# A two-layer decoder trunk in float32 on one core: down products summed onto x in PSUM, ordinary work by readiness, held transposes, reused banks

## The chip, the core and the metric

The kernel runs on one core of a Trainium2 chip. The core has TensorE for matmuls (PE in the profile, its weight loads PEld), VectorE (DVE), ScalarE (ACT), GpSimd (POOL) and SyncE (SP), which issues most DMAs here. Each engine runs its own instructions in order and waits for the others by semaphores. Matmuls write to PSUM, which has eight banks of 128 partitions x 512 float32; the other data lie in SBUF. The metric is the time of one execution on the device in microseconds; a kernel's figure is the median of its runs. A profiled execution gives the trace. Its span runs from the first instruction of the program to the last.

## The reference

256 tokens (two blocks of 128), width 2048, two layers. Each layer:

```
h = rms_norm(x, norm1_g);  z = h @ w_in                    # 2048 x 3584
out_a = chunked_sgu(gelu(z[:, :2048]), ...)                # spatial gate in chunks of 128
out_b = swa_sink_attention(q, k, v, ..., sinks, rel_bias)  # window of 128
x = x + concat(rms_norm(out_a), rms_norm(out_b)) @ w_out
h2 = rms_norm(x, norm2_g)
x = x + (silu(h2 @ w_gate) * (h2 @ w_up)) @ w_down         # 2048 x 5632, 5632 x 2048
```

All is float32.

## The kernel before

Every weight matrix is read from memory once, in loads of 256 x 512 float32 (`raw`, 512 KB, six buffers, issued by SP). A load is split into two float32r parts: ACT casts it to `wh` (L95), DVE subtracts to get `wl` (L96). The activations are kept in split form too (`hT`, `aT`, `ext`: tiles with a high and a low half). A product of a weight piece is three matmuls of 128 x 128 by 512 (`mm3`, L133: high x high, high x low, low x high), added in a PSUM bank; `first` sets `start`, by which the bank is begun anew.

The part around the change is the feed-forward of each layer. The 5632 gate and up columns are 11 blocks of 512. Nine of them (`S_BLOCKS`, 2 to 10) go through `seven` (L564): a two by two block product made of seven products instead of eight. Its halves are token block and row parity; DVE makes sums of weight pieces (L590, L591, L596), and one sum is completed by a DMA from GpSimd that adds to its destination (L598). The seven products are summed in banks of the pool `pa` (five buffers): `m0` to `m4` first, in half units of six matmuls (`s_unit`), then, after ACT and DVE have combined those banks in SBUF (L606 to L615), two more in newly taken banks `n0` and `n1` (L618), which DVE adds to `m1` and `c21` (L628). Silu and a product give the two result tiles `sg`.

Blocks 0 and 1 go through `gate_up` (L651), two ordinary products of eight units each (a unit is one load and 12 matmuls, L138). `down` (L666) multiplies finished blocks by `w_down`: for each of four columns of 512 it sums the units of its blocks in two PSUM banks, one per token block (`dacc`, the only two buffers of pool `pd`; banks of `pa` once the last seven-product block is through), and DVE adds the banks to the residual `xres` in SBUF (L685). In the last layer the last such addition is followed by the DMA to the output; in the first layer the last one is followed by the next layer's norm (`norm_block`).

A finished block's `sg` tiles (pool `zp`, tag `z`, eight buffers) are turned for `down` by `act_T` (L550): four transposes on PE into one bank, a copy on ACT (L554) and a subtraction on DVE (L555) give one of two `aT` tiles (eight buffers). `later(delay, fn)` puts such work off until the counter `clock` has gone on by `delay`; a unit counts 1, a half unit 0.5.

The order of the two kinds of work is planned when the program is built. `debt` counts DVE's work in microseconds (`vec`: 1.14 for a split or a sum, 0.6 for a PSUM operation) less PE's (`pe`: 0.227 per matmul times `LOAD`). After each step of the seven-product stream the ordinary stream goes on while `debt` is positive (L701 to L703). The ordinary stream is a written list, `STD_ORDER` (L43). Where a `down` lacks the transposed tiles of one of its blocks it yields `False` (L669), and only seven-product work goes on. When the seven-product blocks are through, the rest of the ordinary stream runs alone. The framework orders each engine's instructions by these priorities and by its own estimate of when they are ready, so neighbours may change places.

Of the kernel before, what the change touches and what calls it, by code (L numbers as in the profile page):

```python
# [16 lines left out]
ALU = mybir.AluOpType  # L17
# [34 lines left out]

# [12 lines left out]
def trunk(ctx, tc, x, xt, w_in, w_out, w_gate, w_up, w_down, sgu_w, sgu_g, consts,  # L65
# [39 lines left out]
    def vec(n, cost=VEC):  # L105
        debt[0] += n * cost
# [7 lines left out]
    def later(delay, fn):  # L114
        pending.append((clock[0] + delay, next(serial), fn))
# [8 lines left out]
    def new_acc(pool=pa, tag="acc"):  # L124
        return [pool.tile([P, NB], F32, tag=tag, name=f"{tag}{t}") for t in range(NTOK)]
# [7 lines left out]
    def mm3(acc, ah, al, wh, wl, first, last):  # L133
        nc.tensor.matmul(acc, ah, wh, start=first, stop=False)  # L134
        nc.tensor.matmul(acc, ah, wl, start=False, stop=False)  # L135
        nc.tensor.matmul(acc, al, wh, start=False, stop=last)  # L136

    def unit(src, acts, acc, first, last):  # L138
        raw = raw_load(src, 2 if clock[0] < 4 else 1)
        wh, wl = split2(raw)  # L140
        for j in range(2):
            act, aj = acts[j]
            for t in range(NTOK):
                ts = slice(t * P, (t + 1) * P)
                mm3(
                    acc[t], act[:, 0, aj, ts], act[:, 1, aj, ts], wh[:, j, :], wl[:, j, :],
                    first and j == 0, last and j == 1,
                )
        pe(12)
        tick()  # L150
# [100 lines left out]
    for lay in range(L):  # L251
# [298 lines left out]
        def act_T(b, c, sg, pairs_f=pairs_f):  # L550
            ps = pm.tile([P, 2, SEQ], F32, tag="sm", name="ps_f")
            transpose_pair([sg[t][:, 2 * c * P : (2 * c + 2) * P] for t in range(NTOK)], ps)
            pair = tp.tile([P, 2, 2, SEQ], F32R, tag="aT", name="aT")
            nc.scalar.copy(pair[:, 0], ps)  # L554
            nc.vector.tensor_tensor(pair[:, 1], ps, f(pair[:, 0]), ALU.subtract)  # L555
            vec(1, VEC_P)
            pe(2)
            pairs_f.setdefault(b, []).append(pair)

        def act_later(b, sg, act_T=act_T):  # L560
            for c in range(2):
                later(2 + c, lambda c=c: act_T(b, c, sg))

        def seven(b, lay=lay, pairs2=pairs2, ext2=ext2, act_later=act_later):  # L564
            bank = [pa.tile([P, NB], F32, tag="acc", name=f"m{i}") for i in range(5)]

            def s_unit(raw, m, i, op, first, last):
                wh, wl = split2(raw)
                for j in range(2):
                    ah, al = (op(2 * i + j, h) for h in range(2))  # L570
                    mm3(bank[m], ah, al, wh[:, j, :], wl[:, j, :], first and j == 0, last and j == 1)
# [34 lines left out]
            m1 = zp.tile([P, NB], F32, tag="z", name="m1")  # L606
            nc.scalar.copy(m1, bank[0])
            u1 = zp.tile([P, NB], F32, tag="z", name="u1")
            nc.vector.tensor_tensor(u1, bank[3], m1, ALU.add)
            c22 = zp.tile([P, NB], F32, tag="z", name="c22")  # L610
            c21 = zp.tile([P, NB], F32, tag="z", name="c21")
            nc.vector.tensor_tensor(c21, bank[2], u1, ALU.add)
            nc.vector.tensor_tensor(c22, bank[1], c21, ALU.add)
            nc.vector.tensor_tensor(u1, bank[1], u1, ALU.add)
            nc.vector.tensor_tensor(u1, bank[4], u1, ALU.add)  # L615
# [10 lines left out]
            sg = [m1, c21]  # L626
            for t, m in ((0, m1), (1, c21)):
                nc.vector.tensor_tensor(m, bank[t], m, ALU.add)  # L628
                nc.scalar.activation(m, m, AF.Silu, scale=rstd2[t])
            for t, c in ((0, u1), (1, c22)):  # L630
                nc.vector.scalar_tensor_tensor(sg[t], c, nrstd2[t], sg[t], ALU.mult, ALU.mult)
            vec(4, VEC_P)
            act_later(b, sg)
            yield

# [27 lines left out]
            vec(NTOK, VEC_P)  # L663
            act_later(b, sg)

        def down(blocks, final, lay=lay, pairs_f=pairs_f, norm_block=norm_block, ss1=ss1, pairs1=pairs1):  # L666
            for n in range(ND):
                while any(len(pairs_f.get(b, [])) < 2 for b in blocks):
                    yield False  # L669
                acc = new_acc() if seven_done[0] else new_acc(pd, "dacc")  # L670
                for k, b in enumerate(blocks):
                    for c in range(2):
                        pair = pairs_f[b][c]
                        unit(
                            w_down[lay, b, n, c], [(pair, 0), (pair, 1)], acc,
                            k == 0 and c == 0, k == len(blocks) - 1 and c == 1,
                        )
                        yield True
                for t in range(NTOK):
                    parts = 2 if final and lay == L - 1 and n == ND - 1 else 1  # L680
                    w = NB // parts
                    for i in range(parts):
                        cs = slice(n * NB + i * w, n * NB + (i + 1) * w)
                        xs = xres[:, t, cs]
                        nc.vector.tensor_tensor(xs, acc[t][:, i * w : (i + 1) * w], xs, ALU.add)  # L685
                        if final and lay == L - 1:
                            nc.sync.dma_start(out[t * P : (t + 1) * P, cs], xs)
                    vec(1, VEC_P)
                if final and lay < L - 1:
                    norm_block(n, ss1, pairs1, lay + 1, C_G1)  # L690

        def std_stream(gate_up=gate_up, down=down):
            for k, (kind, what) in enumerate(STD_ORDER):
                if kind == "gu":
                    yield from gate_up(what)
# [102 lines left out]
```

## Time and profile before

| | us |
|---|---|
| median of 3 runs | 1981.08 |
| lowest, highest | 1977.15, 1983.19 |
| profiled execution | 1970.47 |
| its span | 1968.8 |
| matmuls, share of the span | 99% |
| ACT, share of the span | 60% |
| DVE, share of the span | 85% |

The granted clock of TensorE was 1.0 over the span. The shares of the slices show where the phases lie (each digit is a tenth of busy time in a fortieth of the span, 49 us):

```profile
PE   9999999999999999999999999999999999999999
DVE  6665689999999999999856666899999999999996
ACT  7565566555565565565656755665656555655563
DMA  9544557667767668668555355576686776686684
```

The stretches in which DVE has 8 or 9 are the two feed-forward phases, about 297 to 960 and 1277 to 1940 us. Rows of groups are read so: line, engine, operation, out<-in by the program's names, shape, count | busy time, mean of one in ns | idle time of the engine just before them, and what ended most of it. A matmul's end is modelled.

### The profile page before, as it was taken

The page shows a single profiled execution, that of the slowest core. Times are in us where ns is not written, and L with a number is a line of the kernel's source. Part 1 is how long each engine was busy: PE and PEld are TensorE (multiplying, and loading weights), DVE is VectorE, ACT ScalarE, POOL GpSimd, SP SyncE. Part 2 cuts the span into 40 slices and gives each one's busy share as a digit, 9 for nine tenths or more (in the row PEclk, how much of TensorE's full clock was granted, in tenths as well). Part 3 has the DMA queues.
Part 4 walks back from the last instruction along what each step waited for, and adds up shares of the span by engine and source line. Part 5 has one row for each costly group of instructions (what it writes and reads, how often), then busy time and mean ns, then how long its engine had stood idle before and what let it go on. Part 6 is the DMA issues. An engine that isn't in the chain of part 4 may idle for free.

```text
span 1968.8 us, 24956 instructions
## 1 busy us (share of the span) xinstructions
PE 1942.7 (99%) x8884; PEld 1586.9 (81%) x8884; DVE 1678.4 (85%) x1812; ACT 1175.8 (60%) x1489; POOL 115.5 (6%) x116
## 2 busy tenths in 40 slices
PE   9999999999999999999999999999999999999999
PEld 6788888778887878888887888878788878888887
DVE  6665689999999999999856666899999999999996
ACT  7565566555565565565656755665656555655563
POOL 0210000000000000000002000000000000000000
PEclk9999999999999999999999999999999999999999
DMA  9544557667767668668555355576686776686684
GB/s 354 188 144 153 189 171 243 206 204 245 231 220 244 221 212 258 220 223 259 202 202 195 127 170 178 178 253 193 214 258 213 225 254 206 210 279 203 221 270 141
DMA packets 117805, 422.20 MB, mean 214 GB/s; under 512 B 13104, under 2 KB 13744, under 8 KB 117680
## 3 DMA queue, kind: packets, MB, share of 16 engines
q1 hardware_dynamic: 105264, 375.52, 53.2%
q0 software_dynamic: 12416, 45.09, 12.3%
q8 instruction: 69, 1.13, 0.2%
q14 instruction: 56, 0.46, 0.1%
HBM read 418.47 MB, written 2.10 MB: 214 GB/s over the span
## 4 chain that ended last, share of the span: by engine, by line
PE 85%; DVE 6%; issue 3%; ACT 2%; DMA 2%; POOL 1%; SPq 0%; DVEq 0%; ACTq 0%; POOLq 0%
PE dacc L134 9%; PE dacc L135 9%; PE dacc L136 9%; PE acc L135 8%; PE acc L136 8%; PE acc L134 8%; PE m L135 7%; PE m L136 7%; PE m L134 7%; PE n L135 3%; PE n L136 3%; PE n L134 3%; DVE wl L96 3%; ACT wh L95 1%; DVE raw L596 1%
## 5 line engine op out<-in xcount | busy, mean ns | idle before, releaser
L95 ACT CAST wh<-raw 128x1024 fp32r<-128x1024 f32 (+1 forms) x778 | 799.9, 1049 | 627.4 <-DVE raw L590 227.3
L96 DVE TENSOR_TENSOR wl<-raw,wh 128x1024 fp32r<-128x1024 f32 (+1 forms) x778 | 927.0, 1217 | 154.5 <-PE acc L135 75.9
L134 PE MATMUL dacc<-wh,aT 128*128 128x512 f32 x608 | 237.0, 392 | 0.2
L135 PE MATMUL dacc<-wl,aT 128*128 128x512 f32 x608 | 237.0, 390 | 0.0
L136 PE MATMUL dacc<-wh,aT 128*128 128x512 f32 x608 | 236.7, 390 | 0.0
L135 PE MATMUL m<-wl,ext 128*128 128x512 f32 x576 | 227.5, 395 | 4.7 <-DVE wl L96 4.7
L134 PE MATMUL m<-wh,ext 128*128 128x512 f32 x576 | 226.8, 394 | 4.8 <-ACT wh L95 4.8
L136 PE MATMUL m<-wh,ext 128*128 128x512 f32 x576 | 224.5, 390 | 0.0
L96 DVE TENSOR_TENSOR wl<-t,wh 128x1024 fp32r<-128x1024 f32 x144 | 175.5, 1219 | 16.0 <-issue 7.0
L95 ACT CAST wh<-t 128x1024 fp32r<-128x1024 f32 x144 | 151.4, 1051 | 49.5 <-PE dacc L136 31.6
L134 PE MATMUL acc<-wh,hT 128*128 128x512 f32 x448 | 179.4, 403 | 0.8 <-ACT wh L95 0.6
L135 PE MATMUL acc<-wl,hT 128*128 128x512 f32 x448 | 176.4, 394 | 1.2 <-DVE wl L96 1.1
L136 PE MATMUL acc<-wh,hT 128*128 128x512 f32 x448 | 175.6, 392 | 0.0
L598 POOL DMA_DIRECT2D t<-in_w_gate_dram x72 | 61.6, 855 | 1373.3 <-DVE wl L96 719.4
L134 PE MATMUL acc<-wh,aT 128*128 128x512 f32 x352 | 139.1, 395 | 0.0
L136 PE MATMUL acc<-wh,aT 128*128 128x512 f32 x352 | 137.3, 390 | 0.0
L135 PE MATMUL acc<-wl,aT 128*128 128x512 f32 x352 | 137.3, 390 | 0.0
L134 PEld LDWEIGHTS dacc<-wh,aT 128*128 128x128 f32 x608 | 114.1, 188 | 25.6 <-DVE xres L685 2.3
L135 PEld LDWEIGHTS m<-wl,ext 128*128 128x128 f32 x576 | 108.1, 188 | 32.0 <-DVE wl L96 10.7
L135 PEld LDWEIGHTS dacc<-wl,aT 128*128 128x128 f32 x608 | 114.2, 188 | 24.1 <-DVE wl L96 0.8
L136 PEld LDWEIGHTS dacc<-wh,aT 128*128 128x128 f32 x608 | 114.2, 188 | 23.7
L134 PEld LDWEIGHTS m<-wh,ext 128*128 128x128 f32 x576 | 108.2, 188 | 29.8 <-ACT wh L95 7.7
(145 smaller groups left out, 2974.3 us busy)
## 6 DMA issues: line engine op xcount, KB each, us to landing
raw<-in_w_gate_dram SPq DMA_DIRECT2D x176, 512.0 KB, 5.4
raw<-in_w_up_dram SPq DMA_DIRECT2D x176, 512.0 KB, 4.2
raw<-in_w_down_dram SPq DMA_DIRECT2D x176, 512.0 KB, 4.9
raw<-in_w_in_dram SPq DMA_DIRECT2D x108, 512.0 KB, 4.1
t<-in_w_gate_dram POOLq DMA_DIRECT2D x72, 512.0 KB, 5.9
raw<-in_w_out_dram SPq DMA_DIRECT2D x64, 512.0 KB, 3.3
bias<-in_band_dram POOLq DMA_DIRECT2D x8, 512.0 KB, 4.9
xr<-in_xt_dram SPq DMA_DIRECT2D x8, 256.0 KB, 6.1
```

Source lines behind the costliest of these rows:

```text
L95: nc.scalar.copy(wh[:, j : j + step, :], src)
L96: nc.vector.tensor_tensor(wl[:, j : j + step, :], src, f(wh[:, j : j + step, :]), ALU.subtract)
L134: nc.tensor.matmul(acc, ah, wh, start=first, stop=False)
L135: nc.tensor.matmul(acc, ah, wl, start=False, stop=False)
L136: nc.tensor.matmul(acc, al, wh, start=False, stop=last)
L596: nc.vector.tensor_tensor(b12, b12, b22, ALU.add)
L598: nc.gpsimd.dma_start(t2, w_gate[lay, b, i, 1], accum_op=ALU.add)
```

## The change

Six things change, the first four in the feed-forward alone:

- Residual: at the start of each column of `down`, ACT copies `xres` into the two banks, and the column's matmuls are added onto it (`start` never set); at the end ACT copies the banks back to `xres`. DVE's addition goes.
- Order: `STD_ORDER` goes. The ordinary stream runs a `down` on up to three blocks whenever two or more are fully transposed (or all that remain are), else the next `gate_up`, else yields. `LOAD` goes from 0.95 to 0.93.
- Held transposes: at most eight `aT` tiles are live; a block's transposes wait in `held` until the last column of a `down` gives tiles back.
- Used banks: the last two of the seven products are added onto banks 0 and 2, so `n0`, `n1` and one addition go, and half units 2 and 4 change places.
- `raw` has seven buffers instead of six.
- The scratch of GpSimd's DMAs (`dynamic_dma_scratch_size`) is 4096 instead of 8192.

```diff
-STD_ORDER = (
-    ("gu", 0), ("down", (0, 2)), ("gu", 1), ("down", (1, 3, 4)), ("down", (5, 6, 7)), ("down", (8, 9)), ("down", (10,)),
-)
+GU_BLOCKS = tuple(b for b in range(NFF) if b not in S_BLOCKS)
+CHUNK = (2, 3)
+ACT_TILES = 8
-LOAD = 0.95
+LOAD = 0.93
...
-        raw = wp.tile([P, 2, NB], F32, tag="raw", name="raw", bufs=6)
+        raw = wp.tile([P, 2, NB], F32, tag="raw", name="raw", bufs=7)
...
+        held = []
+        live = [0]
+
+        def release(live=live, held=held, act_T=act_T):
+            while held and live[0] < ACT_TILES:
+                live[0] += 1
+                act_T(*held.pop(0))
+
-        def act_later(b, sg, act_T=act_T):
+        def act_later(b, sg, held=held, release=release):
             for c in range(2):
-                later(2 + c, lambda c=c: act_T(b, c, sg))
+                def ready(c=c):
+                    held.append((b, c, sg))
+                    release()
+
+                later(2 + c, ready)
...
+                s_unit(b22, 4, i, e_op(3), first, last)
+                yield
                 s_unit(b12, 2, i, e_op(0), first, last)
                 yield
-                s_unit(b22, 4, i, e_op(3), first, last)
-                yield
                 kept.append(t2)
...
+            nc.scalar.copy(m0, bank[0])
+            nc.vector.tensor_tensor(m0, bank[3], m0, ALU.add)
+            nc.vector.tensor_tensor(c12, bank[1], m0, ALU.add)
+            nc.vector.tensor_tensor(c12, bank[4], c12, ALU.add)
+            nc.vector.tensor_tensor(c21, bank[2], m0, ALU.add)
             nc.vector.tensor_tensor(c22, bank[1], c21, ALU.add)
...
-            bank = [pa.tile([P, NB], F32, tag="acc", name=f"n{i}") for i in range(2)]
             for i in range(4):
                 b21 = raw_load(w_gate[lay, b, i, 1])
-                first, last = i == 0, i == 3
-                s_unit(b21, 0, i, a_op(1, 0), first, last)
+                s_unit(b21, 0, i, a_op(1, 0), False, i == 3)
                 yield
-                s_unit(kept[i], 1, i, a_op(1, 1), first, last)
+                s_unit(kept[i], 2, i, a_op(1, 1), False, i == 3)
                 yield
...
+            nc.vector.tensor_tensor(m0, bank[2], m0, ALU.add)
+            sg = [zp.tile([P, NB], F32, tag="z", name="sg0"), m0]
+            for t, c in ((0, bank[0]), (1, m0)):
+                nc.scalar.activation(sg[t], c, AF.Silu, scale=rstd2[t])
...
+        left = [NFF]
+
+        def down(blocks, lay=lay, pairs_f=pairs_f, norm_block=norm_block, ss1=ss1, pairs1=pairs1, left=left, live=live, release=release):
+            left[0] -= len(blocks)
+            final = left[0] == 0
             for n in range(ND):
-                while any(len(pairs_f.get(b, [])) < 2 for b in blocks):
-                    yield False
                 acc = new_acc() if seven_done[0] else new_acc(pd, "dacc")
+                for t in range(NTOK):
+                    nc.scalar.copy(acc[t], xres[:, t, n * NB : (n + 1) * NB])
                 for k, b in enumerate(blocks):
                     for c in range(2):
...
+                        if n == ND - 1:
+                            live[0] -= 1
+                            release()
                         yield True
...
-                        nc.vector.tensor_tensor(xs, acc[t][:, i * w : (i + 1) * w], xs, ALU.add)
+                        nc.scalar.copy(xs, acc[t][:, i * w : (i + 1) * w])
...
+            gus = list(GU_BLOCKS)
+            downed = set()
+            while left[0]:
+                full = [b for b in sorted(pairs_f) if len(pairs_f[b]) == 2 and b not in downed]
+                rest = left[0] == len(full)
+                if len(full) >= CHUNK[0] or rest:
+                    blocks = full[: CHUNK[1]]
+                    downed.update(blocks)
+                    yield from down(blocks)
+                elif gus:
+                    yield from gate_up(gus.pop(0))
                 else:
-                    yield from down(what, k == len(STD_ORDER) - 1)
+                    yield False
...
-    nc = bacc.Bacc("TRN2", target_bir_lowering=False, num_devices=1, dynamic_dma_scratch_size=8192)
+    nc = bacc.Bacc("TRN2", target_bir_lowering=False, num_devices=1, dynamic_dma_scratch_size=4096)
```

More of the change, by code (lines that the diff above doesn't have):

```diff
@@ L131, in small_ps, with mm3, unit @@
         return pool.tile(shape, F32, tag=tag, name=name)
[L133 to L138, printed above, removed]
+    def mm3(acc, ah, al, wh, wl, first, last, again=False):
+        nc.tensor.matmul(acc, ah, wh, start=first, stop=False, skip_group_check=again)
+        nc.tensor.matmul(acc, ah, wl, start=False, stop=False, skip_group_check=again)
+        nc.tensor.matmul(acc, al, wh, start=False, stop=last, skip_group_check=again)
+    def unit(src, acts, acc, first, last, again=False):
         raw = raw_load(src, 2 if clock[0] < 4 else 1)
@@ L146, in unit @@
                     acc[t], act[:, 0, aj, ts], act[:, 1, aj, ts], wh[:, j, :], wl[:, j, :],
-                    first and j == 0, last and j == 1,
+                    first and j == 0, last and j == 1, again,
                 )
@@ L558, in act_T, with s_unit @@
             pairs_f.setdefault(b, []).append(pair)
-        def act_later(b, sg, act_T=act_T):
+        held = []
[5 more added lines that the diff above has]
+        def act_later(b, sg, held=held, release=release):
             for c in range(2):
-                later(2 + c, lambda c=c: act_T(b, c, sg))
+                def ready(c=c):
+                    held.append((b, c, sg))
+                    release()
+                later(2 + c, ready)
         def seven(b, lay=lay, pairs2=pairs2, ext2=ext2, act_later=act_later):
             bank = [pa.tile([P, NB], F32, tag="acc", name=f"m{i}") for i in range(5)]
-            def s_unit(raw, m, i, op, first, last):
+            def s_unit(raw, m, i, op, first, last, bank=bank):
                 wh, wl = split2(raw)
@@ L570, in s_unit @@
                     ah, al = (op(2 * i + j, h) for h in range(2))
-                    mm3(bank[m], ah, al, wh[:, j, :], wl[:, j, :], first and j == 0, last and j == 1)
+                    mm3(
+                        bank[m], ah, al, wh[:, j, :], wl[:, j, :], first and j == 0,
+                        last and j == 1, m in (0, 2),
+                    )
                 pe(6)
@@ L600, in seven @@
                 yield
+                s_unit(b22, 4, i, e_op(3), first, last)
+                yield
                 s_unit(b12, 2, i, e_op(0), first, last)
                 yield
-                s_unit(b22, 4, i, e_op(3), first, last)
-                yield
                 kept.append(t2)
[L606 to L609, printed above, removed]
@@ L610, in seven @@
-            c22 = zp.tile([P, NB], F32, tag="z", name="c22")
-            c21 = zp.tile([P, NB], F32, tag="z", name="c21")
-            nc.vector.tensor_tensor(c21, bank[2], u1, ALU.add)
+            m0, c12, c21, c22 = (
+                zp.tile([P, NB], F32, tag="z", name=v) for v in ("m0", "c12", "c21", "c22")
+            )
+            nc.scalar.copy(m0, bank[0])
+            nc.vector.tensor_tensor(m0, bank[3], m0, ALU.add)
+            nc.vector.tensor_tensor(c12, bank[1], m0, ALU.add)
+            nc.vector.tensor_tensor(c12, bank[4], c12, ALU.add)
@@ L623, in seven @@
                 yield
-                s_unit(kept[i], 1, i, a_op(1, 1), first, last)
+                s_unit(kept[i], 2, i, a_op(1, 1), False, i == 3)
                 yield
[L626 to L630, printed above, removed]
+            nc.vector.tensor_tensor(m0, bank[2], m0, ALU.add)
+            sg = [zp.tile([P, NB], F32, tag="z", name="sg0"), m0]
@@ L631, in seven @@
+            for t, c in ((0, bank[0]), (1, m0)):
+                nc.scalar.activation(sg[t], c, AF.Silu, scale=rstd2[t])
+            for t, c in ((0, c12), (1, c22)):
                 nc.vector.scalar_tensor_tensor(sg[t], c, nrstd2[t], sg[t], ALU.mult, ALU.mult)
-            vec(4, VEC_P)
+            vec(3, VEC_P)
             act_later(b, sg)
@@ L664, in gate_up @@
             act_later(b, sg)
-        def down(blocks, final, lay=lay, pairs_f=pairs_f, norm_block=norm_block, ss1=ss1, pairs1=pairs1):
+        left = [NFF]
+        def down(blocks, lay=lay, pairs_f=pairs_f, norm_block=norm_block, ss1=ss1, pairs1=pairs1, left=left, live=live, release=release):
+            left[0] -= len(blocks)
+            final = left[0] == 0
             for n in range(ND):
-                while any(len(pairs_f.get(b, [])) < 2 for b in blocks):
-                    yield False
                 acc = new_acc() if seven_done[0] else new_acc(pd, "dacc")
+                for t in range(NTOK):
+                    nc.scalar.copy(acc[t], xres[:, t, n * NB : (n + 1) * NB])
                 for k, b in enumerate(blocks):
@@ L675, in down @@
                             w_down[lay, b, n, c], [(pair, 0), (pair, 1)], acc,
-                            k == 0 and c == 0, k == len(blocks) - 1 and c == 1,
+                            False, k == len(blocks) - 1 and c == 1, True,
                         )
+                        if n == ND - 1:
+                            live[0] -= 1
+                            release()
                         yield True
+                last = final and lay == L - 1
+                parts = 2 if last and n == ND - 1 else 1
+                w = NB // parts
                 for t in range(NTOK):
-                    parts = 2 if final and lay == L - 1 and n == ND - 1 else 1
-                    w = NB // parts
                     for i in range(parts):
@@ L684, in down, with std_stream @@
                         xs = xres[:, t, cs]
-                        nc.vector.tensor_tensor(xs, acc[t][:, i * w : (i + 1) * w], xs, ALU.add)
-                        if final and lay == L - 1:
+                        nc.scalar.copy(xs, acc[t][:, i * w : (i + 1) * w])
+                        if last:
                             nc.sync.dma_start(out[t * P : (t + 1) * P, cs], xs)
-                    vec(1, VEC_P)
                 if final and lay < L - 1:
                     norm_block(n, ss1, pairs1, lay + 1, C_G1)
[L692 to L695, printed above, removed]
+        def std_stream(gate_up=gate_up, down=down, pairs_f=pairs_f, left=left):
+            gus = list(GU_BLOCKS)
[9 more added lines that the diff above has]
+                    yield from gate_up(gus.pop(0))
                 else:
-                    yield from down(what, k == len(STD_ORDER) - 1)
+                    yield False
         other = std_stream()
```

2 lines of the change are left out of this document (removed).

## The prediction

> **What bounds the kernel now.** I read the busy shares first, then the two long stretches in which the gated product and the down product run (a "feed-forward phase" per layer), then the pauses in them.
>
> ```profile
> PE 1942.7 (99%) x8884; PEld 1586.9 (81%) x8884; DVE 1678.4 (85%) x1812; ACT 1175.8 (60%) x1489; POOL 115.5 (6%) x116
> ```
>
> TensorE's matmul row is full to 1.3%. By the view of time windows (length, then busy time and count of PE, PEld, DVE, ACT, POOL):
>
> ```profile
> 297.00:960.00 663.00, 656.19 (x2908) 535.98 (x2907) 629.38 (x614) 397.18 (x422) 29.86 (x35) 1.00 0.72 230
> 1277.00:1940.00 663.00, 656.85 (x2912) 536.86 (x2912) 629.77 (x615) 397.97 (x423) 29.87 (x35) 1.00 0.72 230
> 420.00:540.00 120.00, 120.00 (x536) 98.63 (x535) 112.87 (x109) 70.73 (x76) 5.11 (x6) 1.00 0.68 217
> 392.00:406.00 14.00, 12.16 (x55) 9.29 (x54) 13.83 (x15) 8.52 (x11) 1.70 (x2) 1.00 0.65 186
> 588.00:604.00 16.00, 13.92 (x65) 10.72 (x64) 15.90 (x18) 9.92 (x13) 1.71 (x2) 1.00 0.60 161
> 1373.00:1387.00 14.00, 11.93 (x53) 8.88 (x53) 13.84 (x15) 8.53 (x11) 1.70 (x2) 1.00 0.57 176
> 1568.00:1584.00 16.00, 13.92 (x65) 10.67 (x64) 15.90 (x18) 10.02 (x12) 1.71 (x2) 1.00 0.62 171
> ```
>
> The first two rows are the phases: PE is idle 6.8 and 6.2 us in them, 13.0 in all. The third is a stretch with no idle. The last four hold 1.84 + 2.08 + 2.07 + 2.08 = 8.1 us of the 13.0, with DVE at 99%: there DVE is the bound. Elsewhere in the phases DVE is near 95% and PE full. What PE waited for inside one of them (timeline of PE):
>
> ```profile
> 595.62 0.27 PE L199 MATMUL ps_f<-ident,sg 128*128 128x128 f32 x1
> 596.44 0.49 PE L134 MATMUL m<-wh,ext 128*128 128x512 f32 x1 [0.54 <-ACT wh L95]
> 597.70 0.50 PE L135 MATMUL m<-wl,ext 128*128 128x512 f32 x1 [0.77 <-DVE wl L96]
> 598.04 0.39 PE L136 MATMUL m<-wh,ext 128*128 128x512 f32 x1
> 598.27 0.40 PE L134 MATMUL m<-wh,ext 128*128 128x512 f32 x1
> ```
>
> A matmul is shown 0.39 us long, but the next starts 0.23 us after it, so each pause is shown about 0.16 us too short. The Trainium skill ("Perfetto Trace Analysis", Identifying the Most-Contended Engine) says so more generally: the matmul row is a bad measure of nearness to the limit, the share of weight loads a better one. Taken alone, 81% would look like 19% of room; the stretch without idle has 98.63 / 120 = 82.2%, so the trace does not agree with that much.
>
> At 82.2% the weight loads of the two phases would take 535.98 / 0.822 = 652 and 536.86 / 0.822 = 653 us, which leaves 21 us of room; the four windows would then hold 2.7 + 3.0 + 3.2 + 3.0 = 11.9. So the whole room is 13 to 21 us, about 1%: the change neither adds nor removes a matmul, so nothing larger can be won by it in these phases.
>
> **The change part by part.**
>
> *Ordinary work by readiness.* The written order makes the ordinary stream stand still when `down((0, 2))` and `down((1, 3, 4))` come up right behind a `gate_up` whose transposes are still due 2 and 3 units later: `yield False`. I stepped the planner's sums by its own rule (1.14 per split or sum, 0.6 per PSUM operation, minus 0.227 x LOAD per matmul). Before: after 41 and again after 115 half units of a layer, six half units follow with no ordinary unit. Each half unit is 6 matmuls, 1.36 us of PE, while DVE's split of it takes 1.22 us (the row below) and the sums as much again. These are the four windows: the `ps_f<-ident,sg` in the rows above is that `gate_up`'s transpose. After: with one full block at the end of the first `gate_up`, the second one starts at once; behind it blocks 0, 2 and 3 are full and the first down runs on them. The stepped order is (0,2,3), (1,4,5), (6,7), (8,9), (10), with no such standstill.
>
> ```profile
> L96 DVE TENSOR_TENSOR wl<-raw,wh 128x1024 fp32r<-128x1024 f32 x774 | 924.3, 1219 | 152.7 <-PE acc L135 75.9 <-issue 34.6 <-ACT wh L95 21.0
> ```
>
> The work there is moved, not saved, but PE's total is fixed, so the idle goes: between 8.1 (as shown) and 11.9 (by weight loads); I take 10, between the two since each of the dozen pauses is shown 0.16 us short.
>
> Counted over a layer: a seven-product block leaves 51.6 - 172 x 0.2111 = 15.3 of debt and an ordinary unit repays 1.39 (before 15.1, 1.45, and 1.2 more debt for each finished column), so 101 of the 120 ordinary units run beside the nine blocks instead of 108, and 19 instead of 12 behind them. The 12 are confirmed by the trace:
>
> ```profile
> L134 PE MATMUL acc<-wh,aT 128*128 128x512 f32 x352 | 139.1, 395 | 0.0
> L685 DVE TENSOR_TENSOR xres<-dacc,xres 128x512 f32<-128x512 f32 x60 | 39.3, 682 | 0.5 <-PE dacc L136 0.2
> L685 DVE TENSOR_TENSOR xres<-acc,xres 128x512 f32<-128x512 f32 x18 | 12.3, 687 | 10.3 <-PE acc L136 10.3
> L685 DVE TENSOR_TENSOR xres<-acc,xres 128x256 f32<-128x256 f32 x4 | 1.4, 418 | 4.1 <-PE acc L136 4.1
> L628 DVE TENSOR_TENSOR m<-n,m 128x512 f32<-128x512 f32 x18 | 12.3, 682 | 0.0
> ```
>
> (352 less the 64 x 4 of the output projection is 96, four for a unit: 24 units in two layers.) The seven units moved behind cost nothing, since a stretch of ordinary units is bound by PE: 12 matmuls against one split.
>
> *Residual by PSUM.* DVE loses 39.3 + 12.3 + 1.4 = 53.0 us. ACT gets a copy in and a copy out for each half column: five down calls, four columns, two token blocks, two layers. No row shows SBUF to PSUM. The nearest:
>
> ```profile
> L554 ACT CAST aT<-ps_f 128x512 fp32r<-128x512 f32 x44 | 25.7, 583 | 20.1 <-PE ps_f L199 11.6 <-PE dacc L136 8.6
> L459 ACT CAST hT<-g 128x512 fp32r<-128x512 f32 x16 | 10.0, 623 | 0.5
> L656 ACT ACTIVATE sg<-dacc,ir 128x512 f32<-128x512 f32 x8 | 5.3, 688 | 4.6 <-PE dacc L136 4.6
> L134 PEld LDWEIGHTS dacc<-wh,aT 128*128 128x128 f32 x608 | 114.1, 188 | 25.6 <-DVE xres L685 2.3
> L134 PEld LDWEIGHTS dacc<-wh,hT 128*128 128x128 f32 x256 | 47.9, 188 | 12.8 <-ACT wh L95 2.4 <-ACT sg L656 0.7
> ```
>
> Out: 0.58 (L554, from PSUM); in: 0.58 to 0.62, I take 0.60. About 80 x 0.58 + 80 x 0.60 = 94 us, which brings ACT from 60% to 65%: no bound. The price is in the turn of a bank. A down column in the phase has only the two `dacc` banks, so column n+1 waits until column n is out. Before, its first bank came free 0.68 us after PE was done; now after out, out, in = 1.76, that is 1.1 later, and the casts of the next units stand behind these copies on ACT, DVE's splits behind the casts, PE behind both. By the stepping there are 13 such turns per layer, 26. They cost nothing while PE has half units ready; without that cover 1.1 each, 28.6 us. From below: the 2.3 us that L685 holds PE now goes too. The nearest rows: four turns behind ACT's Silu (L656) held PE 0.7 us, 0.18 each. I take 0.2 each, 5.2, less 2.3 = 2.9 lost. What speaks for a small price is that ACT may be late without harm; it waited 2.75 and 1.62 us for PE at two starts of L554, and in the window around them PE lost nothing (timeline of ACT, then the window):
>
> ```profile
> 706.94 0.59 ACT L554 CAST aT<-ps_f 128x512 fp32r<-128x512 f32 x1 [2.75 <-PE dacc L136]
> ...
> 711.05 0.59 ACT L554 CAST aT<-ps_f 128x512 fp32r<-128x512 f32 x1 [1.62 <-PE dacc L136]
> ...
> 704.00:716.00 12.00, 12.00 (x55) 9.91 (x56) 11.37 (x14) 6.21 (x8) 0.37 (x1) 1.00 0.91 279
> ```
>
> At the end of the kernel four half copies on ACT replace four adds of 0.42 us on DVE in front of the output's DMAs: within 0.2 us, nothing. SP's queue has these DMAs at the same places as before, the next loads behind them.
>
> *Held transposes* put a block's transposes off until fewer than eight `aT` tiles live; the L554 waits above are what they act on, hidden already. Where one is released, ACT's copy waits for the unit just issued, as in the last window: nothing on PE. Two `z` tiles per held block stay in use; the stepping has at most four held at once.
>
> *Products onto used banks.* One addition fewer per block (L628, 12.3 us in all), no banks `n`; the half units 4 and 2 change places, so that bank 2's sum is the fourth of five DVE operations, and two to three ordinary units and a half unit stand before the product that needs it. Nothing on PE.
>
> *Seven raw buffers.* The chain of waits has single loads of 7 us on it, issued only when a buffer came free:
>
> ```profile
> 368.50 0.36 ACT aT L554
> 368.86 7.08 DMA raw<-in_w_up_dram
> 376.04 1.06 ACT wh L95
> 377.14 0.50 PE dacc L134
> ```
>
> One more buffer issues each load a unit earlier. With the freed DVE time (65 us) it acts on the idle outside the four windows: 4.9 us as shown, 8.8 by weight loads. I take 3; the ends are 0 and 8.8. POOL's half scratch: its 72 accumulating loads stand far apart (POOL 6% busy), nothing.
>
> **Sum:** -10 - 3 + 2.9 = -10.1 us. The profiled execution took 1970.47 us, of which 1968.8 are the span; it would become 1960.4. The median of the runs is 1981.1, so 10.6 more than the profiled one; the same difference gives **1971.0**.
>
> **Rivals.**
>
> 1. *As summed*, 1966 to 1977.
> 2. *All the room is won*: turns hidden altogether (-2.3) and up to 15.7 of the 21 us: -18, 1963. For it: DVE would have 4% more slack everywhere. Against: some pauses lie at the phases' beginning, where no stock has been made yet.
> 3. *No change*: the pauses leave the four windows and come back at the 26 turns, at 0.5 to 0.6 us each: 26 x 0.55 - 2.3 = 12 against 13 won, 1980. For it: splits are ready shortly before PE needs them in these phases, and every turn puts 2.4 us of copies ahead of the next cast.
> 4. *Slower*: at each turn PE finds no half unit ready, and the whole 1.1 us shows: 28.6 - 2.3 - 13 = +13, 1994. It decides from 0.59 us a turn on; beyond 0.82 the loss exceeds 0.3%. Against it: window 704 to 716, and L656.
>
> **Numbers.** Chances: 0.45, 0.12, 0.26, 0.17. A measurement of this kernel tells 0.3% (5.9 us) from no change, so faster means under 1975.1 and slower over 1987. Faster: 0.41 of the first, the second, 0.03 of the third, 0.56. Slower: 0.15 of the fourth, rounded up to 0.16. The rest is 0.28. Range: 1960 (the second, less the runs' 3 us of scatter) to 1992, just short of the fourth's full price. The forecast's own range is 1966 to 1977.
>
> **What would show it.** Readiness right: no pair of windows per layer with DVE at 99% and PE idle by 2 us; PE idle in the phases under 6 us. Turns right: PE's waits for ACT's copies under 6 us in all, ACT near 65%, DVE near 82%. Loads right: no 7 us load in the chain. It would be wrong if PE's first matmul of a column waits half a microsecond or more for ACT in most turns, if DVE idles behind casts, or if the ordinary stream stands still elsewhere for want of full blocks.

## The result and the profile after

| | us |
|---|---|
| changed kernel, median of 4 runs | 1952.36 (1951.71 to 1953.42) |
| kernel before, beside it | 1979.99 (1977.15 to 1983.19) |
| ratio | 0.9861, 95% interval 0.9843 to 0.9878 |
| profiled execution after, and its span | 1952.96, 1951.2 |
| profiled execution before, and its span | 1970.47, 1968.8 |

The change is faster by 1.4%. Between the two medians lie 27.6 us, between the two profiled executions 17.5. The forecast was 10. Both differences matter below: the second is what the first traces can account for, the first is what the kernel gained.

The busy row of the changed kernel's page:

```profile
PE 1936.5 (99%) x8884; PEld 1587.5 (81%) x8884; DVE 1624.8 (83%) x1712; ACT 1253.2 (64%) x1651; POOL 115.3 (6%) x116
```

The same 8884 matmuls. DVE's row is 53.6 us shorter and ACT's 77.4 longer. Instructions of one engine overlap a little in the trace, so these rows show less than the sum of the instructions' own durations, which fell by 64.5 on DVE and rose by 93.9 on ACT: the 65 and 94 of the forecast. The windows of the two feed-forward phases, then the two stretches in which the transposes behind a `gate_up` now fall in the first layer:

```profile
297.00:960.00 663.00, 662.29 (x2948) 543.80 (x2947) 612.65 (x578) 434.86 (x495) 29.88 (x35) 1.00 0.75 233
1277.00:1940.00 663.00, 662.43 (x2948) 544.06 (x2947) 607.73 (x567) 434.07 (x493) 29.89 (x35) 1.00 0.73 229
389.00:403.00 14.00, 14.00 (x67) 11.57 (x67) 13.10 (x14) 7.14 (x9) 0.84 (x1) 1.00 0.83 257
484.00:500.00 16.00, 16.00 (x76) 13.22 (x75) 13.60 (x15) 10.30 (x13) 0.00 (x0) 1.00 0.65 220
```

PE's idle time in the phases went from 13.0 to 0.7 + 0.6 = 1.3 us. By weight loads at 82.2% (543.80 / 0.822 = 661.6 and 544.06 / 0.822 = 661.9) the room went from 21 to about 2.5. So what the first trace showed as room has been won nearly to the end, and DVE has slack (612.65 and 607.73 busy of 663, before 629 and 630). Who held PE's weight loads, and what ACT waited for among the loads from memory (waits from 297 to 1940 us, that is the phases and what lies between them):

```profile
PEld dacc L135 <- DVE wl L96: 6.8, 18, 0.4
PEld m L135 <- DVE wl L96: 2.3, 4, 1.0
...
PEld dacc L134 <- ACT dacc L686: 2.0, 6, 0.4
...
ACT wh L95 <- DMA raw<-in_w_down_dram: 2.2, 4, 0.8
...
ACT wh L95 <- DMA raw<-in_w_gate_dram: 0.6, 1, 0.6
```

The columns are microseconds in all, times, and the longest. The new copies (L686 in, L705 out) hold PE 2.0 us in all; the adds of before held it 2.3. ACT waited 2.8 us for loads; in the first profile of before it was 25.6:

```profile
ACT wh L95 <- DMA raw<-in_w_down_dram: 19.9, 20, 2.7
...
ACT wh L95 <- DMA raw<-in_w_up_dram: 4.3, 4, 1.4
...
ACT wh L95 <- DMA raw<-in_w_gate_dram: 1.4, 1, 1.4
```

### The profile page after: what moved, and what is told of

The parts are those of the page before. It is cut to its first block, busy times and chain, and to the rows that moved or that the text cites. A ratio compares the mean times of both kernels' runs of the same rounds, so it can differ in the third digit from the quotient of the medians.

```text
span 1951.2 us, 24946 instructions
## 1 busy us (share of the span) xinstructions
PE 1936.5 (99%) x8884; PEld 1587.5 (81%) x8884; DVE 1624.8 (83%) x1712; ACT 1253.2 (64%) x1651; POOL 115.3 (6%) x116
## 4 chain that ended last, share of the span: by engine, by line
PE 91%; DVE 3%; issue 3%; ACT 1%; DMA 1%; POOL 1%; SPq 0%; ACTq 0%; DVEq 0%; POOLq 0%
PE m L135 11%; PE m L136 11%; PE m L134 11%; PE dacc L135 10%; PE dacc L134 10%; PE dacc L136 10%; PE acc L135 8%; PE acc L136 8%; PE acc L134 8%; DVE wl L96 1%; PE ps_f L199 1%; POOL ir L182 1%; PE ps_v L372 1%; PE ps_n L199 1%; ACT s L349 0%
## 5 line engine op out<-in xcount | busy, mean ns | idle before, releaser
L135 PE MATMUL dacc<-wl,aT 128*128 128x512 f32 x576 | 225.9, 392 | 0.0
L136 PE MATMUL dacc<-wh,aT 128*128 128x512 f32 x576 | 225.0, 391 | 0.0
L134 PE MATMUL dacc<-wh,aT 128*128 128x512 f32 x576 | 224.3, 394 | 0.1
L134 PE MATMUL m<-wh,hT 128*128 128x512 f32 x432 | 168.4, 390 | 0.0
L136 PE MATMUL m<-wh,hT 128*128 128x512 f32 x432 | 168.3, 389 | 0.0
L135 PE MATMUL m<-wl,hT 128*128 128x512 f32 x432 | 168.3, 389 | 0.0
L134 PE MATMUL acc<-wh,aT 128*128 128x512 f32 x384 | 151.5, 395 | 0.0
L136 PE MATMUL acc<-wh,aT 128*128 128x512 f32 x384 | 150.1, 391 | 0.0
L135 PE MATMUL acc<-wl,aT 128*128 128x512 f32 x384 | 149.7, 390 | 0.0
L135 PEld LDWEIGHTS dacc<-wl,aT 128*128 128x128 f32 x576 | 108.2, 188 | 26.4 <-DVE wl L96 4.7
L134 PEld LDWEIGHTS dacc<-wh,aT 128*128 128x128 f32 x576 | 107.8, 188 | 25.2 <-ACT dacc L686 2.0
```

The costliest lines, as they stand in the source:

```text
L134: nc.tensor.matmul(acc, ah, wh, start=first, stop=False, skip_group_check=again)
L135: nc.tensor.matmul(acc, ah, wl, start=False, stop=False, skip_group_check=again)
L136: nc.tensor.matmul(acc, al, wh, start=False, stop=last, skip_group_check=again)
```

## The experiments

Runs of one group share the runs of the kernel before on the same chip. "Difference" is median less the median of before in the group; the changed kernel was run again in the second group.

| run | difference, us | ratio to before, 95% interval |
|---|---|---|
| e1 before again | 0.1 | 0.9999 (0.9990 to 1.0008) |
| e2 order and held transposes alone | -16.0 | 0.9917 (0.9903 to 0.9931) |
| e3 residual alone | +5.2 | 1.0022 (1.0011 to 1.0032) |
| e4 changed kernel, written order | -8.3 | 0.9955 (0.9942 to 0.9969) |
| e5 changed kernel | -24.8 | 0.9873 (0.9858 to 0.9888) |
| e6 changed kernel, residual on DVE | +0.5 | 1.0005 (0.9996 to 1.0014) |
| e7 changed kernel, six raw buffers | -14.9 | 0.9921 (0.9908 to 0.9934) |
| e8 changed kernel, banks n again | -24.3 | 0.9877 (0.9862 to 0.9892) |
| e9 as e6, LOAD 0.95 | -14.9 | 0.9925 (0.9913 to 0.9937) |
| e10 seventh raw buffer alone | -10.2 | 0.9953 (0.9941 to 0.9964) |
| e11 changed kernel, LOAD 0.95 | -16.9 | 0.9914 (0.9901 to 0.9928) |
| e12 held transposes alone | -1.5 | 0.9995 (0.9986 to 1.0003) |
| e13 order, held transposes, seventh buffer, halved scratch | -24.5 | 0.9877 (0.9858 to 0.9896) |
| e14 as e6, LOAD 0.945 | -20.8 | 0.9897 (0.9878 to 0.9917) |
| e15 changed kernel, LOAD 0.92 | -22.5 | 0.9891 (0.9871 to 0.9910) |
| e16 halved scratch alone | -0.4 | 0.9997 (0.9986 to 1.0008) |
| e17 changed kernel, eight raw buffers | -21.3 | 0.9889 (0.9875 to 0.9904) |

Some expectations, printed below, missed. e6 fits neither of its two theories, and e9 and e14 lie between theirs. e3, e4, e7 and e17 lie 1 to 4 us outside the range that fits them best, and e15 went the other way, within the intervals. e5 was expected at 1946 to 1950 us and took 1951.9; its four runs lie within 1.6 us of each other, the 17 of before beside it within 6.8.

### e1: the kernel before, again

No edit.

> The kernel before, unchanged. Asked: is the profiled execution's 1970.5 us, 10 us under its median, a lucky one? If the pauses of the two phases vary from execution to execution (theory V), this profile shows a span apart from 1968.8 by several us, with other pauses in the four windows at 392, 588, 1373 and 1568 us. If the trace is the same within 1 us and the runs are again near 1980, the profiled execution is simply shorter than the others for a reason that lies outside the pauses.

Its 11 runs lay between 1973.54 and 1977.54, and the other runs of before in the later groups between 1971.81 and 1984.28. The 1970.47 of the first profile is the shortest execution of before seen at all. This profile took 1977.3, its span 1975.6; the order of PE's instructions is the same. The windows of the phases, and the first layer's two pauses:

```profile
297.00:960.00 663.00, 655.78 (x2904) 535.04 (x2903) 629.67 (x613) 397.52 (x422) 29.85 (x35) 1.00 0.73 230
1277.00:1940.00 663.00, 654.32 (x2887) 531.89 (x2886) 626.60 (x610) 395.45 (x418) 30.83 (x37) 1.00 0.73 229
392.00:406.00 14.00, 12.27 (x55) 9.48 (x55) 13.84 (x15) 8.29 (x10) 1.69 (x2) 1.00 0.67 200
588.00:604.00 16.00, 13.89 (x65) 10.69 (x64) 15.90 (x18) 9.89 (x12) 1.70 (x2) 1.00 0.60 164
```

The two pauses are as before to 0.1 us; the time went elsewhere. PE idles 7.2 + 8.7 = 15.9 instead of 13.0; by weight loads the room is (663 - 650.9) + (663 - 647.1) = 28 instead of 21. The chain of waits tells where: among its longest pieces in the two phases there were three late loads in the first profile (all in the first layer), here there are nine:

```profile
369.74 7.10 DMA raw<-in_w_up_dram
382.68 5.87 DMA raw<-in_w_up_dram
680.47 6.64 DMA raw<-in_w_down_dram
693.10 6.84 DMA raw<-in_w_down_dram
1317.75 7.17 DMA raw<-in_w_gate_dram
1364.02 8.03 DMA raw<-in_w_up_dram
1444.15 7.24 DMA raw<-in_w_down_dram
1602.77 7.46 DMA raw<-in_w_down_dram
1824.04 7.40 DMA raw<-in_w_down_dram
```

So these two standstills are fixed, and the number of loads that come too late differs. The profiles of e12 and e16, which take the time of before, fit this: six such loads in an execution of 1973.7 us, seven in one of 1974.2. The granted clock goes with the time as well. Of the executions of before in these groups, the twelve with a mean granted clock of 0.997 or 0.998 average 1979.6 us, the 31 at 1.000 average 1975.0, and these 31 alone still lie between 1972.7 and 1979.5. How the spread divides between late loads and the clock isn't shown.

### e2, e12, e4: the order

e2 is the kernel before with `held`, `release`, `live` and the new `std_stream`; e12 has the held transposes in the written order; e4 is the changed kernel with

```diff
-            gus = list(GU_BLOCKS)
...
+            for kind, what in STD_ORDER:
+                if kind == "gu":
+                    yield from gate_up(what)
+                else:
+                    while any(len(pairs_f.get(b, [])) < 2 for b in what):
+                        yield False
+                    yield from down(what)
```

> Only the order by readiness with the held transposes in the kernel before; adds on DVE, LOAD 0.95, six raw buffers, banks n as before. Theory S (the standstills of the ordinary stream were the cost): most of the gain, -10 to -20 us against before, no window with PE idle by 2 us behind a gate_up. Theory D (the 65 us taken off DVE are the cause): within 4 us of before, pauses elsewhere instead.

> Only the held transposes, in the kernel before with its written order. I put them at nothing: within 2 us of before. If they are what takes ACT's waits for aT tiles away and these matter: -4 us or more.

> The changed kernel with the written order again (and its standstills); residual by PSUM, held transposes, used banks, LOAD 0.93, seven raw buffers stay. Theory S: +8 to +15 us against the changed kernel, the four windows back with PE idle about 2 us each. Theory D: within 4 us of the changed kernel.

Alone the order and the held transposes gain 16.0 us, the held transposes by themselves nothing that can be told. Back in its written form the order costs the changed kernel 24.8 - 8.3 = 16.5, and the pause at 392 stands in e4's trace again:

```profile
392.00:406.00 14.00, 12.18 (x55) 9.22 (x54) 13.97 (x15) 9.23 (x11) 1.69 (x2) 1.00 0.66 186
```

PE idle 1.82 us there with DVE at 99.8%. The theory of the standstills holds, from both sides: in e4's trace the six stretches of 20 us from 390, 590, 1370, 1570, 430 and 1410 us have 14.7 us of room by weight loads at 82.2% (12.4 in the first four, 2.3 in the last two), in the changed kernel's none, and the two profiled executions are 16.2 us apart. The order by readiness without held transposes wasn't tried.

### e10, e7, e16, e17: the raw buffers

```diff
-        raw = wp.tile([P, 2, NB], F32, tag="raw", name="raw", bufs=6)
+        raw = wp.tile([P, 2, NB], F32, tag="raw", name="raw", bufs=7)
```

e10 makes this edit and halves the scratch in the kernel before, e16 halves the scratch alone; e7 undoes both in the changed kernel, e17 goes to eight buffers.

> Only the seventh raw buffer (and the halved scratch) in the kernel before. Taken out of the changed kernel it cost 10 us. If late loads cost the same beside the standstills: -7 to -10 us against before. If before's loads are late for another reason (they wait for DVE, which is the bound in the four windows): within 3 us.

> The changed kernel with six raw buffers and the scratch of 8192 again. If loads that are issued late made the pauses outside the four windows (my term of 3 us), +3 to +6 us against the changed kernel and a wider spread of its executions; if not, within 2 us.

> The kernel before with GpSimd's scratch of 4096 alone, six raw buffers. The run with the seventh buffer had both and gained 10 us. If the buffer is the cause: within 2 us of before. If the scratch has a part in it: 3 us or more either way.

> The changed kernel with eight raw buffers. ACT's waits for loads in the two phases were 28 us or more with six buffers and under 3 with seven, so there is little left: within 1.5 us of the changed kernel. If loads still set the pauses that are left, -2 us or more.

The buffer gains 10.2 us alone and 24.8 - 14.9 = 9.9 in company; the scratch nothing. Among the longest pieces of e10's chain of waits in the phases no load of this kind is left, and ACT's waits for loads are down to one row:

```profile
ACT wh L95 <- DMA raw<-in_w_down_dram: 4.0, 4, 1.8
```

while e7's are back at 36.6 us:

```profile
ACT wh L95 <- DMA raw<-in_w_down_dram: 29.3, 23, 3.1
...
ACT wh L95 <- DMA raw<-in_w_gate_dram: 4.3, 6, 1.5
...
ACT wh L95 <- DMA raw<-in_w_up_dram: 3.0, 3, 1.4
```

Two of e10's standstills are untouched, so the two gains can add (10.2 and 16.0; e13, which has both, gains 24.5):

```profile
392.00:406.00 14.00, 12.30 (x56) 9.57 (x55) 13.90 (x14) 8.52 (x11) 1.69 (x2) 1.00 0.67 188
588.00:604.00 16.00, 13.98 (x65) 10.73 (x64) 15.90 (x17) 9.93 (x13) 0.94 (x2) 1.00 0.68 164
```

The eighth buffer gains nothing; by the table it is 3.5 us behind the changed kernel, with intervals that overlap. With seven buffers there is nothing left for an eighth: ACT's waits for these loads are 2.8 us with seven and none with eight.

### e3, e6, e9, e14, e13: the residual by PSUM

e3 brings only the copies in and out; e6 takes them out of the changed kernel:

```diff
-                for t in range(NTOK):
-                    nc.scalar.copy(acc[t], xres[:, t, n * NB : (n + 1) * NB])
...
-                            False, k == len(blocks) - 1 and c == 1, True,
+                            k == 0 and c == 0, k == len(blocks) - 1 and c == 1,
...
-                        nc.scalar.copy(xs, acc[t][:, i * w : (i + 1) * w])
+                        nc.vector.tensor_tensor(xs, acc[t][:, i * w : (i + 1) * w], xs, ALU.add)
...
+                    vec(1, VEC_P)
```

e9 and e14 are e6 with LOAD 0.95 and 0.945; e13 is e2 with the seventh buffer and the halved scratch.

> Only the residual by copies into and out of PSUM in the kernel before. Theory S: within 4 us of before, the four windows still there, since the written order still stands still there. Theory D: -8 us or more. If the turns of the banks cost what I feared (0.2 us each at 26 to 28 turns) it is +3.

> The changed kernel with the residual added on DVE again (65 - 12 = 53 us back on DVE). Alone, the residual by PSUM cost 0.2%. Theory P (its price is the same in any company): this is 2 to 5 us faster than the changed kernel. Theory R (it pays once the standstills are gone, since DVE's slack then sets how fast the stock of split weights is made up): 3 to 8 us slower than the changed kernel.

> The changed kernel with the residual added on DVE and LOAD 0.95. The run without the residual at LOAD 0.93 was 25 us slower, but by the planner's sums it also ran out of full blocks: the additions' debt calls for 112 ordinary units beside the nine blocks, and the stream stands still from half unit 214 to 229 and from 244 on; at 0.95 the sums give 102 units and no standstill. Theory S (standstills are the cost, wherever they come from): within 6 us of the changed kernel, near 1955. Theory R (the residual itself is worth it): still 15 us or more slower, 1967 or above.

> The changed kernel with the residual added on DVE and LOAD 0.945: by the planner's sums 106 ordinary units beside the nine blocks and no standstill. Theory O: within 2 us of the changed kernel (1950 to 1954), so that the 9 us by which the run at 0.95 was slower came from its lower count of ordinary units. Theory R: 1957 or more.

> The kernel before with the order by readiness, the held transposes and the seventh raw buffer; additions on DVE, banks n, LOAD 0.95 (108 ordinary units beside the nine blocks, no standstill). Alone these gave -16 and -10 us. If they are the whole of it (theory O: the residual by PSUM and the used banks only pay for each other): -24 to -26 us, as the changed kernel. If the residual is worth something of its own (theory R): -18 us or less, 3 us or more behind the changed kernel.

e3 lost 5.2 us, e6 lost 25.3 against the changed kernel: at first sight the residual is bad alone and worth everything in company. e6's trace says why that reading is wrong. It has new standstills; this is the one at 892 us, in the timeline of PE, with the window's row below (the number behind POOL is the granted clock):

```profile
891.42 0.39 PE L135 MATMUL dacc<-wl,aT 128*128 128x512 f32 x1
891.64 0.39 PE L136 MATMUL dacc<-wh,aT 128*128 128x512 f32 x1
894.86 0.47 PE L134 MATMUL dacc<-wh,aT 128*128 128x512 f32 x1 [2.83 <-DVE xres L703]
...
896.51 0.63 PE L136 MATMUL dacc<-wh,aT 128*128 128x512 f32 x1
896.93 0.63 PE L134 MATMUL dacc<-wh,aT 128*128 128x512 f32 x1
...
```

```profile
892.00:900.00 8.00, 5.17 (x17) 4.11 (x17) 5.14 (x6) 2.43 (x3) 0.00 (x0) 0.79 0.69 236
```

Additions on DVE add to `debt`, and at LOAD 0.93 the planner then asks for 112 ordinary units beside the nine blocks, more than there are full blocks for: stepped through, the stream stands still from half unit 214 to 229 of a layer, and from 244 on. At 0.945 (106 units, no standstill) the same kernel is at -20.8, and at 0.95 (102 units, none) at -14.9. So most of e6's loss comes from the standstills. Part of it is the granted clock behind them: four windows of 8 us (from 892, 960, 1876 and 1944 us) have 0.79. In the first of them eight matmuls took 3.4 us instead of 1.8, so an estimate for the four is 6 us of the 25.

And e13, with the additions on DVE, the banks `n` and LOAD as before, is at -24.5, the changed kernel's -24.8. So the residual by PSUM, the used banks and the lower LOAD together bring nothing that can be told from zero once order and buffer are there. That doesn't make each of them worth nothing in any company. At the same LOAD of 0.95, with used banks, the residual by PSUM makes 2.0 us (e9 -14.9, e11 -16.9, intervals overlap). With the additions on DVE and LOAD 0.95, used banks instead of the banks `n` (e9 against e13) lose 9.6: the addition that they save is also debt that the planner no longer counts, 102 ordinary units instead of 108. e3's loss may have the same reason, though no run isolates it: without the additions' debt the planner asks for 96 ordinary units instead of 108, so DVE has fewer of them in which to catch up.

### e8, e11, e15: banks and LOAD

e8 has `seven` as before in the changed kernel; e11 and e15 change only LOAD.

> The changed kernel with banks n and the extra addition again, half units 2 and 4 in the old order. I put this at nothing: within 2 us of the changed kernel. If the split transposes of before (two and two, with a wait between) come from the longer chain of additions before Silu, they are back here and it is +4 to +8.

> The changed kernel with LOAD 0.95: by the planner's sums 93 instead of 101 ordinary units beside the nine blocks, no standstill either way, but less cover for DVE on the way. If the step of LOAD is only a trim: within 3 us. If DVE's stock of split weights needs it: +5 to +10 us.

> The changed kernel with LOAD 0.92: 106 instead of 101 ordinary units beside the nine blocks, no standstill. LOAD 0.95 (93 units) cost 7 us. If cover for DVE is what counts, 1 to 3 us faster than the changed kernel, or the same where there is no idle left to take.

In the changed kernel the used banks are worth nothing (-24.3 against -24.8). LOAD is not a trim: at 0.95 the changed kernel loses 7.9 us, at 0.92 2.3 (that one within the intervals). By the planner's sums 93, 101 and 106 ordinary units run beside the nine blocks at 0.95, 0.93 and 0.92. The total does not explain the loss, for e9 has 102 and is 9.9 us behind the changed kernel, which has 101. The places explain more: stepped through, the first seven-product block has an ordinary unit after its 8th and one after its 13th half unit at 0.93, and both of these after the 12th at 0.95. The beginnings of the two phases, first in the changed kernel, then in e11:

```profile
300.00:370.00 70.00, 70.00 (x313) 57.23 (x312) 67.13 (x66) 46.60 (x52) 3.42 (x4) 1.00 0.74 226
1280.00:1350.00 70.00, 70.00 (x311) 57.25 (x311) 67.34 (x64) 45.56 (x50) 3.44 (x4) 1.00 0.76 238
300.00:370.00 70.00, 68.40 (x300) 54.43 (x299) 65.10 (x66) 44.99 (x51) 3.42 (x4) 1.00 0.69 218
1280.00:1350.00 70.00, 68.41 (x299) 54.38 (x298) 65.28 (x65) 43.60 (x48) 3.44 (x4) 1.00 0.71 215
```

By weight loads at 82.2% the room there is 0.7 us in the changed kernel and 7.6 in e11 (3.8 and 3.8), and e11 has 25 matmuls fewer there, 5.8 us at 0.23. So most of the 7.9 lies at the beginnings. e9 has 7.6 there too; the first profile of before had 5.9 (2.4 and 3.5). It is not the whole account: e13, at LOAD 0.95 and with a plan that begins as e11's, has 4.8 there and is level with the changed kernel. What it wins elsewhere, these runs do not show.

No version was faster than the changed kernel by more than the intervals; e13 and e8 match it.

## Why the prediction was wrong

The forecast was 1971.0 with a range of 1960 to 1992; measured are 1952.4. The direction was right, and so was the second rival's picture of the profile (all the room won, -18 between the profiled executions, measured -17.5). What failed is the bound on the room, and under it the sizes of three terms of the sum. Step by step:

**The base.** "The profiled execution took 1970.47 us [...]; the same difference gives 1971.0." That execution was the shortest of all that were seen of before. The room of 13 to 21 us was read from it ("nothing larger can be won by it in these phases") and then carried over to a median 10 us higher, as if those 10 us were a constant that the change can't touch. The measured gain between the medians is 27.6, more than all that room. e1 shows 28 us of room in an execution of 1977.3, with nine late loads instead of three. Had the 10.6 been counted as room, the second rival would have stood at 1952.4 instead of 1963, and the lower end of the range near 1949. This is an estimate, and so near a hit is chance, since a part of the 10.6 may be the granted clock.

**Seven raw buffers: the term of 3 us.** The mechanism was right: single loads of 7 us on the chain, issued only when a buffer came free. The size was not: 10.2 alone, 9.9 in company. I let it act only on "the idle outside the four windows" of the one trace, 4.9 to 8.8 us, and took 3 of it. ACT's waits for loads, 25.6 us in all, were in the profile as a sign that more was there; I did not use that row.

**Readiness: the term of 10 us.** Measured 16.0 alone and 16.5 in company, with the four windows gone. The windows hold 8.1 to 11.9. The other 4 to 8 us lie outside the windows that I cut around the pauses. e4's trace has 12.4 by weight loads in the 20 us around them, and another 2.3 in the stretches from 430 and 1410 us, where the forecast had none; the rest these runs do not place.

**Turns of the banks: the term of +2.9.** This was mis-sized as well. The copies cost what was said (L686 0.593 us, L705 0.584, against 0.60 and 0.58):

```profile
L686 ACT COPY dacc<-xres 128x512 f32<-128x512 f32 x56 | 32.7, 593 | 0.8
L705 ACT COPY xres<-dacc 128x512 f32<-128x512 f32 x56 | 32.6, 584 | 30.5 <-PE dacc L136 30.3
```

They hold PE 2.0 us in all instead of the 5.2 set down, against 2.3 by the adds: no loss. ACT waits 30.3 us for PE at the copies out, and does so without harm, as the window at 704 us suggested. The third and the fourth rival, which both needed dear turns, fall with this row.

**Right:** the used banks, the held transposes and the scratch at nothing (e8, e12, e16); DVE near 82% (83%), ACT near 65% (64%); the 19 ordinary units behind the blocks cost nothing. **Not in the sum: what LOAD does by itself.** I costed 0.93 only as part of the counts, at nothing, and held the pauses at the phases' beginning against the second rival. With the residual on PSUM, 0.95 is 7.9 us slower, nearly all of it at these beginnings, where the changed kernel has 0.7 us of room and the first profile of before 5.9. With the residual on DVE, 0.93 brings the ordinary stream to a stand and is 21 us slower than 0.945.

Redone with what was measured, readiness -16 and buffer -10 make -26 of the -27.6. The second rival's -18 fits the profiled executions because both start from the same short one; for the medians it was 9.6 us short as well.

## What to carry to other kernels

Where a planner shares out work by a debt, an operation moved off an engine moves the plan too: step the plan for every variant, and compare where it puts the work as well as how much of it, or a standstill is taken for the price of the operation. Read the room from more than one execution. Take a row of waits for loads as a sign that a buffer is worth trying (25.6 us of waits here, 10 us gained), and not the idle that one trace happens to show. Two gains that remove different waits (here standstills, 16 us, and late loads, 10) add up even on an engine that looks 99% busy.

## What the runs showed of the hardware

A pause of TensorE can be followed by a stretch of lower granted clock. In e6 the pause at 892 us is 3.22 us from the start of one matmul to the next (2.83 shown as idle). From 895.65 to 898.64 us eight matmuls started 0.43 us apart instead of 0.23; the granted clock from 892 to 900 us is 0.79.

The length of the pause alone doesn't decide it. A pause in the first profile of before, 2.72 us from start to start, was followed by no such stretch (timeline of PE); the granted clock from 92 to 96 us is 1.00:

```profile
89.86 0.39 PE L134 MATMUL acc<-wh,hT 128*128 128x512 f32 x1
92.58 0.44 PE L363 MATMUL ps_p<-ident,s 128*128 128x128 f32 x2 [2.33 <-ACT s L349]
92.78 0.48 PE L135 MATMUL acc<-wl,hT 128*128 128x512 f32 x1
93.09 0.39 PE L136 MATMUL acc<-wh,hT 128*128 128x512 f32 x1
```

The same pause in e1, 2.71 us from start to start, was followed by one; the granted clock from 92 to 96 us is 0.64:

```profile
88.95 0.39 PE L134 MATMUL acc<-wh,hT 128*128 128x512 f32 x1
91.66 0.69 PE L363 MATMUL ps_p<-ident,s 128*128 128x128 f32 x2 [2.32 <-ACT s L349]
92.00 0.78 PE L135 MATMUL acc<-wl,hT 128*128 128x512 f32 x1
92.57 0.63 PE L136 MATMUL acc<-wh,hT 128*128 128x512 f32 x1
```

What decides it, no run here shows. The Trainium skill ("TensorE: Matmul & The Clock Gate", HAM oscillation) gives about 3.4 us of idle as the limit; here the lower clock came after 2.83 us shown as idle in e6 and 2.32 in e1.
